# Expert weights: the low parts of every weight piece subtracted on VectorE instead of three in four there and one on GpSimd

## The chip, the core and the metric

One NeuronCore of one Trainium2 chip runs the whole program. The metric is the device time of one execution in microseconds (us). The engines are named as the profile names them: PE is TensorE's matmul, PEld its weight load, DVE is VectorE, ACT is ScalarE, POOL is GpSimd, and SP is SyncE, which here only issues DMAs.

## What is computed

The reference is a two-layer network in float32 on 1024 tokens of width 1024. The part around this change is the mixture of experts of the first layer: a router gives each token two of 32 experts, and each expert is a gated feed-forward net.

```python
hg = lax.ragged_dot(xs, w_gate.astype(xs.dtype), sizes)
hu = lax.ragged_dot(xs, w_up.astype(xs.dtype), sizes)
ys = lax.ragged_dot(jax.nn.silu(hg) * hu, w_down.astype(xs.dtype), sizes)
ys = ys * gates.reshape(-1)[order][:, None].astype(ys.dtype)
y = jax.ops.segment_sum(ys, tok, num_segments=t)
```

`xs` are the tokens of each expert in a row; `w_gate` and `w_up` are 1024 x 512 per expert, `w_down` is 512 x 1024. What comes before (two recurrent mixers, an output projection, the router) and after (the second layer) is not touched.

## The kernel before

**Exact products from rounded halves.** The matrix engine works on numbers in the rounded type F32R. To keep float32's accuracy each operand is split in two: a high part h, the raw number rounded to F32R, and a low part l = raw - h. `split` (lines 109 to 116) does it: ACT makes h by a copy (line 112), and another engine makes l by a subtraction (line 113). A product then takes three matmuls: h by h, h by l, l by h.

**One expert.** `expert` (from line 955) handles up to 128 tokens. POOL clears the tile `X` (line 960) and gathers the expert's tokens into it by an indirect DMA (line 961). PE transposes them (line 969), and `split` gives `XTh` and `XTl`. Each of the three weight matrices is used in four pieces of 512 KB. `wload` (lines 972 to 980) takes the next raw piece that has been loaded, and splits it into `ewh` and `ewl`, each 128 x 1024 with four buffers. Its argument q is the number of the piece in the matrix, 0 to 3. Pieces of the gate and up matrices feed six matmuls each (line 989), pieces of the down matrix too (line 1010). Between, ACT and DVE form silu(gate) * up in `eth` (lines 994 to 996), PE transposes it (line 1001) and it is split into `Hh` and `Hl`. At the end ACT scales the result into `Y` (line 1012), and POOL adds it to the tokens by an indirect DMA (line 1013).

**Who subtracts.** `wload` picks the engine by the piece's number: one of the four pieces of each matrix, three per expert and 96 in all, has its low part made on POOL, the other 288 on DVE.

```python
eng = nc.gpsimd if q == 1 else nc.vector
```

**The stage.** `moe` (from line 1018) runs the 32 experts as generators, one expert's down product beside the next one's gate and up products. The raw pieces are loaded by SP (line 376) in a ring: 19 buffers, seven of which (`eraw`) remain from expert 8 on; a buffer is loaded again when its piece has been split. From expert 8 on the freed memory serves `hyena_filters` (line 1154), work for the second layer that is done beside the experts: a small network's outputs are multiplied with a window on DVE (`hfb`, line 1217), POOL adds and subtracts pairs of them (`hsum`, line 1220, and `hd`, line 1223), the results are split (`hsh` on ACT, `hsl` on DVE, lines 115 and 116), transformed on PE (`dps`), combined on DVE (lines 1284 and 1285), and added and subtracted once more on POOL (`HR` and `HS`, line 1252).

**The order of the work.** No queue is written by hand: the program is recorded, and a scheduler that estimates every instruction sets the order on each engine at build time. A change of one instruction's engine can therefore move others on all five engines. Each engine then works its own queue strictly in order. A last part of `moe` for experts with more than 128 tokens is a loop on the chip that runs only where there are any.

Of the kernel before, what the change touches and what calls it, by code (L numbers as in the profile page):

```python
# [49 lines left out]
class Kern:  # L50
# [904 lines left out]
    def expert(self, ep, psm, pst, pg, gi, gate, wg, wu, wd, next_raw):  # L955


        nc = self.nc
        X = ep.tile([P, D], F32, name="X")
        nc.gpsimd.memset(X, 0.0)  # L960
        nc.gpsimd.indirect_dma_start(out=X, out_offset=None, in_=self.h2_d,
                                     in_offset=bass.IndirectOffsetOnAxis(ap=gi, axis=0),
                                     bounds_check=L - 1, oob_is_err=False)
        XTh = ep.tile([P, 8, P], F32R, name="XTh")
        XTl = ep.tile([P, 8, P], F32R, name="XTl")
        for q in range(2):
            pt = pst.tile([P, 4, P], F32, name="pt")
            for t in range(4):
                nc.tensor.transpose(pt[:, t], X[:, (q * 4 + t) * P:(q * 4 + t + 1) * P], self.ident)
            self.split(XTh[:, q * 4:q * 4 + 4], XTl[:, q * 4:q * 4 + 4], pt)  # L970

        def wload(w, q, down=False):
            shape = [P, D] if down else [P, 2, 512]
            eng = nc.gpsimd if q == 1 else nc.vector
            raw = next_raw(self.piece(w, q, down))
            h = ep.tile(shape, F32R, name="ewh", tag="ewh", bufs=4)
            l = ep.tile(shape, F32R, name="ewl", tag="ewl", bufs=4)
            self.split(h, l, raw, eng=eng)
            return h, l

        yield
        pgu = []
        for w in (wg, wu):
            ps = psm.tile([P, 512], F32, name="pgu", tag="s")
            for q in range(4):
                h, l = wload(w, q)
                for k in range(2):
                    for i, (a, b) in enumerate(((XTh, h), (XTh, l), (XTl, h))):
                        nc.tensor.matmul(ps, a[:, q * 2 + k], b[:, k], start=q == 0 and k == 0 and i == 0,  # L989
                                         stop=q == 3 and k == 1 and i == 2)  # L990
            pgu.append(ps)
            yield
        th = ep.tile([P, 512], F32, name="eth", bufs=1)
        nc.scalar.activation(th, pgu[0], AF.Tanh, scale=0.5)
        nc.vector.scalar_tensor_tensor(th, th, 1.0, pgu[0], op0=ALU.add, op1=ALU.mult)
        nc.vector.tensor_tensor(th, th, pgu[1], op=ALU.mult)
        Hh = ep.tile([P, 4, P], F32R, name="Hh", bufs=1)
        Hl = ep.tile([P, 4, P], F32R, name="Hl", bufs=1)
        pt = pst.tile([P, 4, P], F32, name="pt")
        for t in range(4):  # L1000
            nc.tensor.transpose(pt[:, t], th[:, t * P:(t + 1) * P], self.ident)
        self.split(Hh, Hl, pt)
        yield
        py = pg.tile([P, D], F32, name="g", tag="g")
        for q in range(4):
            h, l = wload(wd, q, True)
            for half in range(2):
                sl = slice(half * 512, half * 512 + 512)
                for i, (a, b) in enumerate(((Hh, h), (Hh, l), (Hl, h))):
                    nc.tensor.matmul(py[:, sl], a[:, q], b[:, sl], start=q == 0 and i == 0, stop=q == 3 and i == 2)  # L1010
        Y = ep.tile([P, D], F32, name="Y", bufs=1)
        nc.scalar.activation(Y, py, AF.Copy, scale=gate)
        nc.gpsimd.indirect_dma_start(out=self.x1_d, out_offset=bass.IndirectOffsetOnAxis(ap=gi, axis=0),
                                     in_=Y, in_offset=None, bounds_check=L - 1, oob_is_err=False,
                                     compute_op=ALU.add)
        yield
# [1285 lines left out]
```

## Time and profile before

| what | us |
|---|---|
| timed runs, median of 3 | 3980.1 |
| timed runs, lowest and highest | 3979.16 and 3992.83 |
| the profiled execution, its own time | 3969.92 |
| span of the profiled execution, first to last instruction | 3967.6 |

The profile is of the profiled execution, which took 2.3 us more than the span of its instructions and 10.2 us less than the median of the timed runs. Times in the rows count from the first instruction. Busy time is the time in which an engine has an instruction running, also where that instruction is held up; "idle before" is the time in which it had none, with what ended it. Durations of neighbouring instructions on DVE and ACT overlap by some hundredths of a us, so that sums of durations lie a few per cent above busy times. The experts' stage reaches from about 1140 us to about 1980 us; in it the experts 0 to 7 run until about 1380 us, the filters' work runs beside the experts from there to about 1900 us, and the last experts run alone again.

### The profile page before, as it was taken

How to read it: one execution, taken by the hardware profiler on the slowest of the kernel's cores; microseconds unless marked ns; L12 is line 12 of the kernel's file. 1: busy time of each engine (PE TensorE's matmuls, PEld its weight loads, DVE VectorE, ACT ScalarE, POOL GpSimd, SP SyncE). 2: the span in 40 equal slices, each digit the busy share in tenths (PEclk: the TensorE clock that was granted, in tenths of full speed). 3: DMA queues.
4: the chain of work that ended last, by engine and by line, in shares of the span. 5: the costliest groups of instructions: out<-in, count | busy, mean ns of one | idle time of the engine just before them, and what ended most of it. 6: DMA issues, size and time to landing. Idle time of an engine off the chain costs nothing. (4 is left out here: it accounts for less than half of the span.)

```text
span 3967.6 us, 52346 instructions
## 1 busy us (share of the span) xinstructions
PE 3544.1 (89%) x19799; PEld 2845.8 (72%) x19799; DVE 2861.4 (72%) x3992; ACT 1503.4 (38%) x2166; POOL 1540.5 (39%) x882
## 2 busy tenths in 40 slices
PE   6999897988978889999879999999776999999897
PEld 6888776666766667777656767887564777888775
DVE  7767858776457889998755887411995577777798
ACT  4332333433226766666633333222123213222331
POOL 4444434553015568777601222000771212223353
PEclk8999997899979999999989999999887999999998
DMA  4222224444568778888854777666556722222521
GB/s 102 96 85 107 97 74 148 137 151 145 182 208 285 233 247 287 294 268 274 280 153 132 213 207 194 185 192 220 161 170 195 258 103 69 85 75 95 177 94 69
DMA packets 540591, 669.34 MB, mean 169 GB/s; under 512 B 151819, under 2 KB 352015, under 8 KB 539824
## 3 DMA queue, kind: packets, MB, share of 16 engines
q1 hardware_dynamic: 429136, 535.38, 42.3%
q10 hardware_dynamic: 101984, 113.79, 8.4%
q0 software_dynamic: 9216, 16.81, 1.9%
q8 instruction: 157, 2.57, 0.3%
q14 instruction: 98, 0.80, 0.1%
HBM read 500.72 MB, written 181.83 MB: 172 GB/s over the span
## 5 line engine op out<-in xcount | busy, mean ns | idle before, releaser
L113 DVE TENSOR_TENSOR ewl<-eraw,ewh 128x1024 fp32r<-128x1024 f32 x243 | 398.8, 1658 | 40.6 <-ACT ewh L112 40.3
L112 ACT CAST ewh<-eraw 128x1024 fp32r<-128x1024 f32 x324 | 334.5, 1049 | 114.1 <-PE pgu L989 51.5
L125 PE MATMUL g<-x2h,wl 128*128 128x512 f32 x688 | 279.2, 406 | 0.0
L125 PE MATMUL g<-x2h,wh 128*128 128x512 f32 x688 | 278.9, 406 | 0.1
L125 PE MATMUL g<-x2l,wh 128*128 128x512 f32 x688 | 277.7, 404 | 0.0
L125 PE MATMUL g<-h,sw 128*128 128x512 f32 (+1 forms) x752 | 243.9, 401 | 20.5 <-ACT sw L112 9.6
L113 POOL TENSOR_TENSOR ewl<-eraw,ewh 128x1024 fp32r<-128x1024 f32 x81 | 215.3, 2658 | 111.1 <-ACT ewh L112 103.0
L163 POOL TENSOR_TENSOR sraw<-sraw 128x1024 f32<-128x1024 f32 x24 | 74.0, 3083 | 431.8 <-DVE sw L113 419.9
L125 PE MATMUL g<-xl,sw 128*128 128x512 f32 x616 | 241.5, 392 | 0.0
L989 PE MATMUL pgu<-ewl,XTh 128*128 128x512 f32 x512 | 210.5, 411 | 28.6 <-POOL ewl L113 18.0
L112 ACT CAST sw<-sraw 128x1024 fp32r<-128x1024 f32 x144 | 148.8, 1048 | 207.0 <-PE g L125 156.2
L125 PE MATMUL g<-z 128*128 128x512 f32 x820 | 201.7, 395 | 22.7 <-DVE z L113 19.7
L125 PE MATMUL g<-sw,h 128*128 128x256 f32 x960 | 184.6, 294 | 22.9 <-DVE sw L113 17.8
L989 PE MATMUL pgu<-ewh,XTh 128*128 128x512 f32 x512 | 204.2, 401 | 0.7 <-ACT XTh L112 0.7
L989 PE MATMUL pgu<-ewh,XTl 128*128 128x512 f32 x512 | 202.8, 396 | 0.0
L125 PEld LDWEIGHTS g<-z 128*128 128x128 f32 x820 | 155.1, 190 | 60.0 <-DVE z L113 23.0
L125 PEld LDWEIGHTS g<-h,sw 128*128 128x128 f32 (+1 forms) x752 | 143.2, 191 | 57.1 <-ACT sw L112 10.5
L113 DVE TENSOR_TENSOR wl<-raw,wh 128x1024 fp32r<-128x1024 f32 x43 | 52.6, 1223 | 173.1 <-ACT wh L112 167.7
L125 PEld LDWEIGHTS g<-sw,h 128*128 128x128 f32 x960 | 158.0, 202 | 23.9 <-DVE sw L113 18.6
L113 POOL TENSOR_TENSOR sw<-sraw,sw 128x1024 fp32r<-128x1024 f32 x39 | 102.5, 2628 | 179.9 <-ACT sw L112 179.9
L499 DVE SCALAR_TENSOR_TENSOR u<-sC,cw,u 128x1023 f32<-128x1023 f32 (+2 forms) x84 | 164.6, 1975 | 1.7 <-ACT u L497 1.4
L193 DVE TENSOR_TENSOR sC<-sU,g 128x512 f32<-128x512 f32 x140 | 95.2, 682 | 89.1 <-PE g L125 86.5
(684 smaller groups left out, 10113.7 us busy)
## 6 DMA issues: line engine op xcount, KB each, us to landing
eraw<-in_exp_w_down SPq DMA_DIRECT2D x112, 512.0 KB, 5.7
eraw<-in_exp_w_up SPq DMA_DIRECT2D x108, 512.0 KB, 4.7
eraw<-in_exp_w_gate SPq DMA_DIRECT2D x104, 512.0 KB, 5.6
sraw<-in_w_in SPq DMA_DIRECT2D x12, 2048.0 KB, 7.8
raw<-in_w_in ACTq DMA_DIRECT2D x43, 512.0 KB, 4.5
SC<-SC SPq DMA_DIRECT2D x32, 512.0 KB, 3.6
cSA<-X SPq DMA_DIRECT2D x32, 512.0 KB, 4.6
cSC<-SC SPq DMA_DIRECT2D x32, 512.0 KB, 7.6
```

What stands on the lines that cost most here:

```text
L112: nc.scalar.copy(h, raw)
L113: (eng or nc.vector).tensor_tensor(l, raw, f32(h), op=ALU.subtract)
L125: nc.tensor.matmul(ps, a, b, start=i == 0, stop=i == n - 1)
L163: Q(A11, A11, A21, op=ALU.subtract)
L193: V(c, x, ps, op=ALU.add)
L499: nc.vector.scalar_tensor_tensor(u[:, j:], x[:, :L - j], cw[:, ct, 3 - j:4 - j], u[:, j:], op0=ALU.mult, op1=ALU.add)
L989: nc.tensor.matmul(ps, a[:, q * 2 + k], b[:, k], start=q == 0 and k == 0 and i == 0, stop=q == 3 and k == 1 and i == 2)
```

## The change

`wload` no longer picks an engine: `split` is called without one, so that all four subtractions of each matrix go to DVE. Nothing else is edited.

```diff
         def wload(w, q, down=False):
             shape = [P, D] if down else [P, 2, 512]
-            eng = nc.gpsimd if q == 1 else nc.vector
             raw = next_raw(self.piece(w, q, down))
             h = ep.tile(shape, F32R, name="ewh", tag="ewh", bufs=4)
             l = ep.tile(shape, F32R, name="ewl", tag="ewl", bufs=4)
-            self.split(h, l, raw, eng=eng)
+            self.split(h, l, raw)
             return h, l
```

Line numbers behind it are lower by one in the changed kernel. The queues of all engines are the same as before up to the start of the experts and from the work after them on; what the scheduler ordered anew lies in the experts' stage.

Two places of the queues follow. The first is DVE's queue around one of the early experts, from its gate pieces to its `Hl` (the numbers tell one buffer's loading from another). Before:

```order
L113 TENSOR_TENSOR ewl<-eraw_9675,ewh 128x1024
L113 TENSOR_TENSOR ewl<-ahead_9699,ewh 128x1024
L113 TENSOR_TENSOR ewl<-ahead_9711,ewh 128x1024
L113 TENSOR_TENSOR XTl<-pt,XTh 128x512
L113 TENSOR_TENSOR ewl<-ahead_9724,ewh 128x1024
L113 TENSOR_TENSOR ewl<-ahead_9748,ewh 128x1024
L113 TENSOR_TENSOR ewl<-ahead_9760,ewh 128x1024
L113 TENSOR_TENSOR Hl<-pt,Hh 128x512
L995 SCALAR_TENSOR_TENSOR eth<-eth,pgu 128x512
L996 TENSOR_TENSOR eth<-eth,pgu 128x512
```

The same place of DVE's queue in the changed kernel:

```order
L113 TENSOR_TENSOR ewl<-eraw_9675,ewh 128x1024
L113 TENSOR_TENSOR ewl<-eraw_9687,ewh 128x1024
L113 TENSOR_TENSOR ewl<-ahead_9699,ewh 128x1024
L113 TENSOR_TENSOR ewl<-ahead_9711,ewh 128x1024
L113 TENSOR_TENSOR XTl<-pt,XTh 128x512
L113 TENSOR_TENSOR ewl<-ahead_9724,ewh 128x1024
L113 TENSOR_TENSOR ewl<-ahead_9736,ewh 128x1024
L113 TENSOR_TENSOR ewl<-ahead_9748,ewh 128x1024
L113 TENSOR_TENSOR ewl<-ahead_9760,ewh 128x1024
L113 TENSOR_TENSOR Hl<-pt,Hh 128x512
L994 SCALAR_TENSOR_TENSOR eth<-eth,pgu 128x512
L995 TENSOR_TENSOR eth<-eth,pgu 128x512
```

The second piece of each four (9687 and 9736) has come into DVE's queue in its turn; `XTl`, `Hl` and the two `eth` keep their places behind the fourth piece.

The second place is POOL's queue in the stretch in which the filters' work runs beside the experts. Before:

```order
L1220 TENSOR_TENSOR hsum<-hfb_13734,hfb_13738 128x256
L1013 DMA x_d<-Y,idx 1024x1024
L113 TENSOR_TENSOR ewl<-eraw_12725,ewh 128x1024
L1252 TENSOR_TENSOR HR<-daC 128x256 x2
L113 TENSOR_TENSOR ewl<-eraw_12774,ewh 128x1024
L1252 TENSOR_TENSOR HR<-dbC,dbS 128x256 x2
L113 TENSOR_TENSOR ewl<-eraw_12907,ewh 128x1024
L960 MEMSET X 128x1024
L1013 DMA x_d<-Y,idx 1024x1024
L961 DMA X<-h_d,idx 128x1024
```

The same place of POOL's queue in the changed kernel:

```order
L1219 TENSOR_TENSOR hsum<-hfb_13734,hfb_13738 128x256
L1012 DMA x_d<-Y,idx 1024x1024
L1251 TENSOR_TENSOR HR<-daC 128x256 x2
L960 MEMSET X 128x1024
L961 DMA X<-h_d,idx 128x1024
L1251 TENSOR_TENSOR HR<-dbC,dbS 128x256 x2
L1012 DMA x_d<-Y,idx 1024x1024
```

POOL keeps the filters' additions, the clearing of `X` and the two indirect DMAs of each expert, and these now stand directly behind one another.

## Rows read from the trace of the kernel before

**Rows 1.** The page, its lines of busy time: us, share of the span, number of instructions.

```profile
PE 3544.1 (89%) x19799; PEld 2845.8 (72%) x19799; DVE 2861.4 (72%) x3992; ACT 1503.4 (38%) x2166; POOL 1540.5 (39%) x882
```

**Rows 2.** Busy time by stretch, all instructions; the first row names the columns.

```profile
core 0: us, PE busy (x) PEld busy (x) DVE busy (x) ACT busy (x) POOL busy (x), PEclk, DMA share, GB/s
...
1170.00:1380.00 210.00, 179.41 (x751) 139.24 (x752) 166.45 (x142) 139.36 (x161) 109.03 (x53) 0.92 0.76 250
1380.00:1900.00 520.00, 485.01 (x2340) 377.40 (x2339) 477.36 (x481) 350.91 (x466) 387.55 (x243) 0.98 0.83 274
1900.00:1980.00 80.00, 69.44 (x317) 54.95 (x315) 57.67 (x52) 51.99 (x58) 45.67 (x21) 0.95 0.83 284
```

**Rows 3.** The same of `ewl` alone: PE, PEld, DVE, POOL, clock, DMA.

```profile
1170.00:1380.00 210.00, 88.31 (x209) 42.34 (x209) 120.83 (x77) 68.80 (x26) 0.92 0.76 250
1380.00:1900.00 520.00, 196.18 (x474) 90.26 (x473) 300.14 (x178) 156.76 (x60) 0.98 0.83 274
1900.00:1980.00 80.00, 35.44 (x86) 16.43 (x86) 47.17 (x32) 27.34 (x10) 0.95 0.83 284
```

**Rows 4.** One instruction's ns, least/median/most: the two engines' `ewl`.

```profile
L113 DVE TENSOR_TENSOR ewl<-eraw,ewh x243: 1202/1214/5149, 1192.0 to 1966.4; 128x1024 fp32r<-128x1024 f32 x122
L113 POOL TENSOR_TENSOR ewl<-eraw,ewh x81: 2343/2447/3454, 1192.0 to 1961.6; 128x1024 fp32r<-128x1024 f32 x81
```

**Rows 5.** The timeline of one early expert: start, us, engine, instruction, idle time before.

```profile
1269.53 1.21 DVE L113 TENSOR_TENSOR ewl<-eraw,ewh 128x1024 fp32r<-128x1024 f32 x1
1271.04 4.15 DVE L113 TENSOR_TENSOR ewl<-eraw,ewh 128x1024 fp32r<-128x1024 f32 x2 [0.30 <-ACT ewh L112]
1275.12 0.68 DVE L113 TENSOR_TENSOR Hl<-pt,Hh 128x512 fp32r<-128x512 f32 x1
...
1269.97 3.01 POOL L113 TENSOR_TENSOR ewl<-eraw,ewh 128x1024 fp32r<-128x1024 f32 x1
...
1275.85 0.50 PE L1010 MATMUL g<-ewh,Hl 128*128 128x512 f32 x1 [2.21 <-DVE Hl L113]
```

**Rows 6.** The timeline beside the filters' work, POOL and DVE.

```profile
1493.31 2.00 POOL L1252 TENSOR_TENSOR HR<-daC 128x256 f32<-128x256 f32 x2
1494.75 2.90 POOL L113 TENSOR_TENSOR ewl<-eraw,ewh 128x1024 fp32r<-128x1024 f32 x1
...
1494.02 4.73 DVE L113 TENSOR_TENSOR ewl<-eraw,ewh 128x1024 fp32r<-128x1024 f32 x1
```

**Rows 7.** `hsl` alone: its DVE busy time by stretch, and one's ns.

```profile
1380.00:1900.00 520.00, 51.93 (x182) 34.63 (x182) 58.93 (x64) 0.98 0.83 274
...
L116 DVE SCALAR_TENSOR_TENSOR hsl<-hsum,hsh x32: 406/604/3342, 1437.3 to 1846.6; 128x256 fp32r<-128x256 f32 x32
```

**Rows 8.** One instruction's ns: the `hsum` (`hd` alike), and `HR`, one of four such rows.

```profile
L1220 POOL TENSOR_TENSOR hsum<-hfb,hfb x32: 718/1584/2238, 1429.2 to 1845.4; 128x256 f32<-128x256 f32 x32
...
L1252 POOL TENSOR_TENSOR HR<-daC x16: 738/1516/1784, 1493.3 to 1876.0; 128x256 f32<-128x256 f32 x16
```

**Rows 9.** PE's waits from 1170 to 1980 us: total, times, longest.

```profile
PE pgu L989 <- POOL ewl L113: 18.0, 12, 5.6
PE g L1010 <- DVE Hl L113: 15.6, 7, 2.8
```

**Rows 10.** What SP's loads waited for from 1170 to 1980 us; POOL's scattered results.

```profile
SPq L376 <- POOL ewl L113: 159.0, 65, 7.5
...
L1013 POOL DMA_INDIRECT x_d<-Y,idx x32: 1561/1995/4905, 1215.1 to 1974.3; - x32
```

**Rows 11.** The timeline of ACT, one result `Y` per expert: experts 1, 6, 28, 30.

```profile
1237.80 1.12 ACT L1012 ACTIVATE Y<-g,gcol 128x1024 f32<-128x1024 f32 x1 [0.31 <-PE g L1010]
...
1351.87 1.11 ACT L1012 ACTIVATE Y<-g,gcol 128x1024 f32<-128x1024 f32 x1
...
1925.69 1.12 ACT L1012 ACTIVATE Y<-g,gcol 128x1024 f32<-128x1024 f32 x1 [0.54 <-PE g L1010]
...
1964.33 1.12 ACT L1012 ACTIVATE Y<-g,gcol 128x1024 f32<-128x1024 f32 x1
```

## The prediction

> **What bounds the kernel now.** The page comes first: over the whole span PE is busy 89%, DVE 72%, POOL 39% [rows 1]. Such averages say little, since the change touches one stage only. So the second view is busy time by stretch, in the three parts of the experts' stage: the early experts (1170 to 1380 us), the middle with the filters' work beside (1380 to 1900), the last experts (1900 to 1980). PE and DVE are high in all three and neither is full: 179.4 and 166.5 of 210 us, then 485.0 and 477.4 of 520, then 69.4 and 57.7 of 80 [rows 2]. The DMA engines are 0.76 to 0.83 busy, ACT at most 0.68. The stage is thus two engines in a chain, PE and DVE, which hold each other up, and in the middle DVE is near its limit: its 42.6 us without work there are spread over 481 instructions.
>
> Third, the same view for `ewl` alone: 26, 60 and 10 of the pieces were subtracted on POOL, and DVE's 77, 178 and 32 took 120.8, 300.1 and 47.2 us [rows 3]. Fourth, how long one takes: on DVE the median is 1.21 us, hardly over the least (1.20), but the longest took 5.15; on POOL it is 2.34 us at best and 2.45 in the median [rows 4]. So most of DVE's subtractions run undisturbed, and some stand still. The timeline says beside what. In an early expert POOL's subtraction runs from 1269.97 to 1272.98; two DVE subtractions that would take 2.4 us take 4.15, end at 1275.19, and `Hl`, queued behind them, makes PE wait 2.21 us [rows 5]. In the middle one DVE subtraction takes 4.73 us, while POOL does two additions for `HR` and then a weight piece, back to back [rows 6]. While one engine runs such an instruction on two SBUF operands, the other's stands.
>
> That is the question of this change: a weight piece on POOL is not free for DVE. What does it cost there, against the 1.21 us that it costs when DVE does it?
>
> **The change, part by part.**
>
> *Added on DVE.* 96 subtractions of 1.21 us: 31.5 us in the early stretch (26), 72.6 in the middle (60), 12.1 in the last (10); one more lies before 1170 us, and one at a border is counted on both sides.
>
> *Returned on DVE.* The lengthening is measured time less undisturbed time. Early: 120.8 - 77 x 1.21 = 27.6 us. Last: 47.2 - 32 x 1.21 = 8.5. Hardly anything else with two operands runs on POOL there, so I give all of it to the moved pieces. Middle: `ewl` 300.1 - 178 x 1.21 = 84.8, and `hsl` 58.9 - 64 x 0.41 = 32.7 [rows 7], together 117.5. This is shared with the filters' own additions on POOL: 32 `hsum`, 32 `hd` and 64 `HR` and `HS`, which hold for about 0.73 us each when nothing delays them [rows 8], 128 x 0.73 = 93 us, against 60 x 2.34 = 140 us of weight pieces. By held time the pieces have 60% of it, 70.5 us. The ends: by the medians, in which POOL's own waiting is counted (32 x 1.58, 32 x about the same, 64 x 1.52, against 60 x 2.45), their share is 42%, 50 us; at most it is all of `ewl`'s own lengthening, 84.8. I take 70.5, since held time is what DVE stands behind. A larger figure, all of the 117.5, is excluded because `HR` is seen at the start of the 4.73 us [rows 6].
>
> *Net on DVE.* Early +4, last +4, and middle 72.6 - 70.5 = **+2** (ends -12 and +23). Early and last DVE has 43.5 and 22.3 us without work, so the 4 us are covered; if that cover goes they are paid. In the middle I count the +2 in full.
>
> *PE's waits.* PE waited 18.0 us, 12 times, for a piece from POOL [rows 9]. A piece then comes after 1.21 us in DVE's queue instead of 2.4 to 3.0 on POOL, but the two pieces behind it are now later in that same queue. I take half, **-9 us** (ends 0 and -18).
>
> *`Hl` in the early experts.* Rebuilt from the timeline: the undisturbed queue runs the first piece to 1270.74, then three of 1.21 us to 1274.37; `Hl` starts there, not at 1275.12, 0.75 us sooner [rows 5]. PE waited for `Hl` 7 times, 15.6 us [rows 9]: 7 x 0.75 = **-5 us** (ends 0 and -15.6).
>
> *What costs nothing.* SP reloads a raw buffer when its piece is split, and waited 159 us for POOL to do so [rows 10]; these waits pass to DVE and get shorter, the loads are the same, and the DMA engines have a sixth to a quarter of their time over [rows 2]. POOL's clearing of `X`, its gathers and scatters and the filters' additions start earlier, since no piece stands before them; nothing that bounds waits for them. ACT gets two more activation-table loads by the new order, covered by its 169 us without work in the middle. The loop for large experts does not run: there are 32 scatters, one per expert [rows 10].
>
> **Sum:** +2 - 9 - 5 = -12 us. The profiled execution would go from 3969.9 to about 3958. It lies 10.2 us below the median of the timed runs, so against those runs I forecast 3980.1 - 12 = **3968 us**. Two independent terms, DVE's (-14, +21 about its value) and PE's (-20, +14), seldom meet their ends together; by the root of the sum of squares this case alone reaches from 3944 to 3993.
>
> **The rivals.**
>
> *Faster: the early experts reach the last ones' pace.* From expert 1 to 6 a result came every (1351.87 - 1237.80) / 5 = 22.8 us; from expert 28 to 30, with the same work and also nothing beside it, every 19.3 [rows 11]. If the early chain is held up by the lengthened subtractions alone, 7 experts gain 3.5 us each, 24.5, in place of the 5 for `Hl`: 3980.1 - 12 + 5 - 24.5 = 3949. For it: the granted clock, 0.92 there and 0.98 in the middle [rows 2], could rise when PE waits less. Against: the last experts had POOL's pieces too, and kept their pace. The Trainium skill, "SBUF — State Buffer", section "SBUF: two separate sides", calls the port pair that DVE and GpSimd share an exclusive lock, held for the whole instruction, behind which the other fully blocks. The trace agrees on the place, not on the amount: if each piece had cost DVE its whole 2.34 us, 140 us would return in the middle where at most 117.5 were lost, and then PE's 35 us without work there would be the most to win.
>
> *Slower: the filters' additions take the place of the weight pieces.* In the middle they lengthen DVE by 117.5 - 70.5 = 47 us now, 0.37 each. Without the pieces in POOL's queue they stand directly behind one another, and meet a DVE whose queue holds a third more subtractions. If every one of the 128 is paid in full, 93 us, DVE loses 46 more, and as it has little time over there the end moves by them: 3968 + 46 = 4014. It is slower than now by 0.5% from 32 us more than my sum, at 0.62 us for each addition. For it: back-to-back POOL instructions already starve a waiting DVE subtraction [rows 6]. Against: DVE also has instructions that read PSUM, beside which an addition runs unseen. A milder form has the same cause: if nothing at all came back, the middle would be charged 72.6 us against the 42.6 that DVE has there, 30 more, 3968 - 2 + 30 = 3996; I give it a twentieth, within this rival, since the lengthened rows are there to see. The Trainium skill, page "Perfetto Trace Analysis", section "Optimizing Scalar/DVE Operations", speaks for this form, and so against the change: where DVE is saturated, moving some of its work to ScalarE or even GpSimd may make sense. It adds that GpSimd and DVE share a read port, so that it might not help, and this caveat is what the trace bears out.
>
> *The change does nothing.* Excluded: the queues show 96 pieces moved.
>
> **How the numbers follow.** About 0.5%, 20 us, is what a measurement of this kernel can tell from no change: 3960 to 4000. My forecast has 0.58; a sixth of it lies below 3960 (0.10), nearly all the rest within. The faster rival has 0.24, of which 0.22 below 3960. The slower has 0.18, of which 0.13 reaches above 4000, and the forecast's upper end lends 0.01. Faster 0.32, same 0.54, slower 0.14. The range takes the forecast's own lower end, which lets out a tenth, and reaches to 4002, leaving a tenth of the slower rival above.
>
> **What would show it.** In the profile after: no `ewl` on POOL and 384 on DVE with a mean near 1.3 us in place of some 1.6; DVE's busy time in the stage within 20 us of before; a stage some 12 us shorter; `Hl`'s waits at about 1.4 us each. A mean of `hsl` still near 0.9, or `ewl` at 1.4 or more, would show the slower rival; 20 us per early expert the faster. My sum is wrong in its base if DVE's busy time falls or grows by over 25 us, and in its PE terms if PE's waits for `ewl` grow by what POOL's were.

## The result, and the profile after

The changed kernel took 3917.97 us in the median of four runs (3910.88 to 3923.73), the kernel before 3979.63 on the same chip: a ratio of **0.9852**, with a 95% interval from 0.9829 to 0.9876. That is 62 us less, or 49 to 68. The forecast was 12 us less, and the result lies below the low end of its range. The two profiled executions differ by less, 3921.0 against 3969.9 us, since that of before lies 10 us under its median and that of after 3 above; what follows accounts for their spans, 3919.2 against 3967.6, so for 48.4 us.

Where they went is read from ACT's timeline, by the result `Y` of the experts 0, 1, 6, 8, 28 and 31 of the changed kernel:

```profile
1210.03 1.12 ACT L1011 ACTIVATE Y<-g,gcol 128x1024 f32<-128x1024 f32 x1 [0.31 <-PE g L1009]
1230.15 1.12 ACT L1011 ACTIVATE Y<-g,gcol 128x1024 f32<-128x1024 f32 x1 [0.31 <-PE g L1009]
...
1333.31 1.10 ACT L1011 ACTIVATE Y<-g,gcol 128x1024 f32<-128x1024 f32 x1
...
1392.07 1.11 ACT L1011 ACTIVATE Y<-g,gcol 128x1024 f32<-128x1024 f32 x1 [0.27 <-PE g L1009]
...
1872.50 1.12 ACT L1011 ACTIVATE Y<-g,gcol 128x1024 f32<-128x1024 f32 x1 [0.57 <-PE g L1009]
...
1919.64 1.11 ACT L1011 ACTIVATE Y<-g,gcol 128x1024 f32<-128x1024 f32 x1 [4.95 <-DMA x_d<-Y,idx]
```

The same results came at 1213.7, 1237.8, 1351.9, 1407.3, 1925.7 and 1972.9 us before ([rows 11] show three of them). So 7.6 us are won by expert 1, 10.9 more from there to expert 6, and 38.0 from expert 8 to expert 28, where the filters' work runs beside; 3.3 are lost between experts 6 and 8, nothing changes over the last three, and the work behind the experts takes 4.9 longer. In other words, an early expert takes 20.6 us instead of 22.8, one in the middle 24.0 instead of 25.9.

The page's line of busy time, against [rows 1]:

```profile
PE 3538.9 (90%) x19799; PEld 2844.4 (73%) x19799; DVE 2834.2 (72%) x4088; ACT 1507.2 (38%) x2168; POOL 1289.0 (33%) x786
```

DVE has 96 instructions more, 116 us of undisturbed work, and is busy 27 us less. Busy time by stretch (columns as in [rows 2]; the middle now ends at 1840 us), all instructions, and below it `ewl` alone with PE, PEld and DVE:

```profile
1170.00:1380.00 210.00, 186.29 (x808) 143.34 (x808) 177.80 (x184) 153.87 (x175) 48.18 (x31) 0.95 0.81 270
1380.00:1840.00 460.00, 452.88 (x2202) 355.05 (x2203) 425.44 (x507) 335.08 (x440) 222.22 (x173) 0.99 0.89 299
```

```profile
1170.00:1380.00 210.00, 91.27 (x224) 43.54 (x224) 130.50 (x109) 0.95 0.81 270
1380.00:1840.00 460.00, 185.56 (x455) 86.43 (x455) 299.06 (x230) 0.99 0.89 299
```

In the middle, before, PE was without work for 35 of 520 us, 6.7% [rows 2]; now for 7.1 of 460, 1.5%. PE has become what bounds this stretch (the run with the piece left out, below, bears on this), and the DMA engines deliver 299 GB/s in place of 274. DVE's 230 subtractions there take 299.1 us, 1.30 each, against 300.1 us for 178, 1.69 each [rows 3]; in the early experts 1.20 against 1.57.

```profile
L113 DVE TENSOR_TENSOR ewl<-eraw,ewh x324: 1202/1218/1811, 1192.5 to 1914.9; 128x1024 fp32r<-128x1024 f32 x162
```

In ns of one, the longest of the `eraw` group fell from 5149 to 1811 [rows 4], the median stayed. `hsl` too is no longer held:

```profile
1380.00:1840.00 460.00, 44.79 (x159) 30.24 (x159) 28.02 (x56) 0.99 0.89 299
```

That is 0.50 us each, against 0.92 [rows 7]. PE's waits from 1170 us to the end of the stage in the changed kernel (total, times, longest), and under them ACT's for `hsum`:

```profile
PE g L1009 <- DVE Hl L113: 12.7, 10, 4.2
...
PE pgu L988 <- DVE ewl L113: 2.3, 2, 1.7
...
PE g L1009 <- DVE ewl L113: 0.4, 1, 0.4
```

```profile
ACT hsh L115 <- POOL hsum L1219: 6.0, 5, 2.3
```

Before, ACT's waits for `hsum` and PE's for low parts were these; PE waited not only for POOL [rows 9] but for DVE as well:

```profile
ACT hsh L115 <- POOL hsum L1220: 29.4, 18, 4.1
```

```profile
PE pgu L989 <- POOL ewl L113: 18.0, 12, 5.6
PE pgu L989 <- DVE ewl L113: 10.3, 12, 2.3
...
PE g L1010 <- DVE ewl L113: 2.2, 2, 1.9
PE g L1010 <- POOL ewl L113: 1.6, 3, 0.8
```

All together PE's 32.1 us went down to 2.7. ACT's waits for `hsum` fell from 29.4 to 6.0 us, those for `Hl` hardly, from 15.6 to 12.7.

### The profile page after: what moved, and what is told of

The parts are those of the page before. It is cut to its first block, busy times and chain, and to the rows that moved or that the text cites. A ratio compares the mean times of both kernels' runs of the same rounds, so it can differ in the third digit from the quotient of the medians.

```text
span 3919.2 us, 52350 instructions
## 1 busy us (share of the span) xinstructions
PE 3538.9 (90%) x19799; PEld 2844.4 (73%) x19799; DVE 2834.2 (72%) x4088; ACT 1507.2 (38%) x2168; POOL 1289.0 (33%) x786
## 5 line engine op out<-in xcount | busy, mean ns | idle before, releaser
L113 DVE TENSOR_TENSOR ewl<-eraw,ewh 128x1024 fp32r<-128x1024 f32 x324 | 415.7, 1306 | 41.6 <-ACT ewh L112 37.6
L125 PE MATMUL g<-z 128*128 128x512 f32 x820 | 201.6, 395 | 22.8 <-DVE z L113 19.7
L125 PE MATMUL g<-sw,h 128*128 128x256 f32 x960 | 185.0, 294 | 22.9 <-DVE sw L113 17.9
L125 PEld LDWEIGHTS g<-h,sw 128*128 128x128 f32 (+1 forms) x752 | 143.4, 191 | 57.5 <-ACT sw L112 10.5
L125 PEld LDWEIGHTS g<-sw,h 128*128 128x128 f32 x960 | 158.4, 202 | 24.0 <-DVE sw L113 18.7
L113 DVE TENSOR_TENSOR sw<-sraw,sw 128x1024 fp32r<-128x1024 f32 x105 | 136.7, 1316 | 34.8 <-ACT sw L112 33.9
L125 PEld LDWEIGHTS g<-x2h,wl 128*128 128x128 f32 x688 | 133.0, 193 | 38.3 <-issue 11.0
```

The costliest lines, as they stand in the source:

```text
L113: (eng or nc.vector).tensor_tensor(l, raw, f32(h), op=ALU.subtract)
L125: nc.tensor.matmul(ps, a, b, start=i == 0, stop=i == n - 1)
```

## The experiments

After the result three things could have carried the gain: that DVE no longer stands beside POOL's subtractions (**standing**), that the piece from POOL came late for PE (**late piece**), and that POOL's own queue is emptier for the filters' additions and the gathers (**queue**). A fourth was the new order that the scheduler made. Each ratio below is against the kernel before on the same chip, with its 95% interval; "changed" is the kernel after the edit.

**An idle subtraction on POOL.** All four pieces are DVE's, as in the changed kernel, and POOL subtracts as before, into a tile that nothing reads.

```diff
             self.split(h, l, raw)
+            if q == 1:
+                d = ep.tile(shape, F32, name="ewd", tag="ewd", bufs=1)
+                nc.gpsimd.tensor_tensor(d, raw, raw, op=ALU.subtract)
```

> The changed kernel, and beside it POOL subtracts each second raw piece from itself into a tile that nobody reads: 96 subtractions as long as the ones that the change took away, on two SBUF operands. All of DVE's subtractions stay on DVE. Theory 1 (standing still): what the change won is the time that DVE stands behind POOL's two-operand instructions. Then DVE's mean ewl goes from 1.31 back to 1.5 us or more, over 100 us of lengthening return on top of the 116 us that DVE now does, and the time comes back to 3980 or above. Theory 2 (the late piece): the win is that PE gets every piece from one queue 1.2 us after its turn, not 2.4 to 3 us late from POOL. No piece comes from POOL here, so the time stays at 3918 within 10 us. Theory 3 (POOL's own queue): the win is that gathers and the filters' additions no longer queue behind pieces. They queue again here, so most of the 62 us return, while DVE's subtractions need not lengthen.

4021.18 us, ratio 1.0107 (1.0074 to 1.0139): some 100 us above the changed kernel, more than the whole gain. DVE's `ewl` from 1140 to 2040 us:

```profile
L113 DVE TENSOR_TENSOR ewl<-eraw,ewh 128x1024 fp32r<-128x1024 f32 x324 | 491.8, 1549 | 15.2 <-ACT ewh L112 14.9
```

1549 ns in the mean, 1306 in the changed kernel, and PE waits for `ewl` from DVE again, 24 us. POOL's subtractions beside all 384 of DVE's cost more than the edit ever won; but POOL's queue is as full as before, so this run alone does not part standing from queue.

**POOL's queue filled with memsets.**

```diff
+            if q == 1:
+                for _ in range(3):
+                    nc.gpsimd.memset(raw, 0.0)
```

> The changed kernel, and POOL clears each second raw buffer three times after its piece is split: 288 memsets of about 0.95 us, 274 us of POOL's time, with no operand read. Theory 1 (standing still): a memset shares little with DVE; the time stays within 3913 to 3935. Theory 2 (the late piece): no piece comes later; 3918 within 10 us. Theory 3 (POOL's own queue): POOL is as full as before the change (255 us of pieces), gathers and additions wait as long, and 30 to 62 us return: 3948 to 3980.

3963.65 us, 0.9969 (0.9951 to 0.9988). DVE was held no more than in the changed kernel (mean 1302), yet most of the gain was gone. The edit did more than was meant: the three memsets keep the raw buffer longer than one subtraction does, and ACT waited 46.6 us for `eraw` from the DMA. Inconclusive; two later runs put the question better.

**Only the lateness.** DVE does every piece; then POOL touches it once more, with a memset of the raw tile and an addition on one column, so that PE has to wait for POOL.

```diff
+            if q == 1:
+                nc.gpsimd.memset(raw, 0.0)
+                l1 = l[:, :1] if down else l[:, 0, :1]
+                r1 = raw[:, :1] if down else raw[:, 0, :1]
+                nc.gpsimd.tensor_tensor(l1, f32(l1), r1, op=ALU.add)
```

> The changed kernel, but the low part of each second piece goes through POOL's queue once more: one memset of its raw buffer (about 0.95 us), then an addition of a cleared number to one column of the low part, so that PE gets the piece about 1.2 us after DVE has made it, as late as when POOL made it. POOL's long two-operand instructions stay away. Theory 1 (standing still): DVE is not held, 3913 to 3935. Theory 2 (the late piece): PE's waits for these pieces come back (19.6 us named on POOL before the change, and what followed from them), 3945 to 3980. Theory 3: a third of the former load on POOL's queue, 3925 to 3940.

3974.49 us, 0.9993 (0.9972 to 1.0014): all of the gain gone, though DVE is held no more than in the changed kernel. `ewl` on DVE, and PE's waits:

```profile
L113 DVE TENSOR_TENSOR ewl<-eraw,ewh 128x1024 fp32r<-128x1024 f32 x324 | 415.1, 1298 | 94.2 <-ACT ewh L112 41.2 <-issue 38.6 <-POOL HS L1256 4.5
```

```profile
PE pgu L993 <- POOL ewl L982: 48.2, 27, 7.5
...
PE g L1014 <- POOL ewl L982: 4.1, 5, 1.5
```

A late piece, with 152 us of POOL's queue taken as well, can thus cost as much as the whole change won. By the medians the delay is that of before: a memset of 0.95 us and an addition of 0.26 come behind DVE's subtraction, 1.21 us, where POOL's subtraction of before was 2.45 - 1.21 = 1.24 us later than DVE's [rows 4]. Its tail is long, though, since the addition is itself held at times; its mean is 0.65 us and its longest 4.07:

```profile
L982 POOL TENSOR_TENSOR ewl<-ewl,eraw x81: 183/262/4072, 1192.5 to 1964.7; 128x1 fp32r<-128x1 f32 x81
```

**The edit for the early experts alone.**

```diff
-            eng = nc.gpsimd if q == 1 else nc.vector
+            eng = nc.gpsimd if q == 1 and self.mid else nc.vector
...
+                self.mid = e >= 8
```

> The kernel before, with the change for the experts 0 to 7 alone; from expert 8 on, beside the filters' work, the second piece stays on POOL. Theories 1 and 2: the early experts keep the changed kernel's pace, 20.4 us instead of 22.8, and win about 18 us: 3962 of 3980, the middle stays as it was. Theory 3: POOL has no filters' additions early, so its queue matters only for the gathers; the win there would be below 8 us, and the larger part lies in the middle.

3967.29 us, 0.9971 (0.9953 to 0.9988). Early experts take 20.66 us each, as changed, and middle ones 26.26, close to the 25.9 of before: each stretch follows its own share of the edit. By this run the early experts hold a fifth of the gain (0.29% of 1.48%), by the changed kernel's own trace more, 18.5 of 48.4 us.

**One more buffer for the split pieces**, on the kernel before and on the changed one. If a late piece hurts because PE has none in hand, a fifth buffer should give the kernel before a third to a half of the gain.

```diff
-            h = ep.tile(shape, F32R, name="ewh", tag="ewh", bufs=4)
-            l = ep.tile(shape, F32R, name="ewl", tag="ewl", bufs=4)
+            h = ep.tile(shape, F32R, name="ewh", tag="ewh", bufs=5)
+            l = ep.tile(shape, F32R, name="ewl", tag="ewl", bufs=5)
...
-                fw4 = w.tile([64, 2, 256], F32, name="fw4")
+                fw4 = w.tile([64, 2, 256], F32, name="fw4", bufs=1)
```

> The kernel before, with five buffers instead of four for the high and the low parts of the pieces (the room comes from one buffer of the filters' weights fw4). POOL still makes three pieces of each expert. Theory 1 (standing still): DVE stands as long as before, 120 us beside POOL's pieces, so 3970 to 3980. Theory 2 (the late piece): with one more piece in store PE does not run out when one comes 1.2 us late; PE's waits for POOL's pieces (19.6 us) fall below 8 and a third to a half of the change's win comes without it, 3945 to 3960.

> The changed kernel with the same fifth buffer. Theory 1: DVE bounds the middle, more store gives it no time: 3910 to 3920. Theory 2: no late piece is left, so the store has nothing to cover either: 3908 to 3920. A larger gain, below 3900, would say that jitter of another kind (the waits for Hl, ACT's casts behind PE) still holds the chain up in the changed kernel.

On the kernel before 4027.36 us, 1.0099 (1.0066 to 1.0132): slower. PE's waits for POOL's pieces did fall to 7.3 us, but those for DVE's rose to 28.4, and the work behind the experts grew from 1994.7 to 2019.7. On the changed kernel 3913.85, 0.9819 (0.9787 to 0.9850): the experts end 21 us sooner, and the work behind them takes 2018.8 us instead of 1999.6. Both were ordered anew by the scheduler, so neither settles what a late piece costs.

**The queue filled again, with no raw buffer kept.** One column of the raw tile is copied, and three memsets go to a tile of their own.

```diff
+            if q == 1:
+                d = ep.tile([P, D], F32, name="ewd", tag="ewd", bufs=1)
+                nc.gpsimd.tensor_copy(d[:, :1], raw[:, :1] if down else raw[:, 0, :1])
+                for _ in range(3):
+                    nc.gpsimd.memset(d, 0.0)
```

> The second run again without its side effect (there the cleared raw buffers came free late, and ACT waited 46.6 us for loads): POOL copies one column of each second raw piece into a tile of its own and clears that tile three times. POOL is as full as before the change, no raw buffer is held, no piece comes late, DVE does not stand. Theories 1 and 2: 3915 to 3930. Theory 3 (POOL's own queue): the filters' additions and the gathers wait, ACT's waits for hsum go from 6 back to some 25 us, and 20 to 40 us return: 3938 to 3958.

3947.83 us, 0.9915 (0.9889 to 0.9941), so about 25 us above the changed kernel. ACT waits 22.5 us for the `hsum` again. By its expectation this is the queue's sign. POOL was filled with more than it had before, though, 359 us of memsets and copies against some 253 us of pieces [rows 3], so this is an upper figure for the queue.

**The filters' additions on DVE too.**

```diff
-                    nc.gpsimd.tensor_tensor(s_, hf[0], hf[1], op=ALU.add)
+                    nc.vector.tensor_tensor(s_, hf[0], hf[1], op=ALU.add)
...
-                    nc.gpsimd.tensor_tensor(hd[:, b], hf[0], hf[1], op=ALU.subtract)
+                    nc.vector.tensor_tensor(hd[:, b], hf[0], hf[1], op=ALU.subtract)
...
-        self.nc.gpsimd.tensor_tensor(out, x, y, op=op)
+        self.nc.vector.tensor_tensor(out, x, y, op=op)
```

> The changed kernel, with the filters' 128 additions and subtractions (hsum, hd, HR, HS) on DVE too. DVE gains 128 x 0.41 = 52 us of work and loses the 34 us that it still stands beside them: +18 us. Theory 1, with DVE as the bound of the middle: 3930 to 3940. Theory 2: the work comes from one queue in its turn, nothing waits for another engine: 3915 to 3930.

> The eighth run's kernel on the chip of the run before it, for the difference: 3900 to 3915, ratio about 0.981.

3908.97 us, 0.9808 (0.9781 to 0.9835), and in a second run of the same kernel 3906.91, 0.9839 (0.9801 to 0.9876). `ewl`'s mean falls to 1219 ns, which is the undisturbed value. By the ratios this kernel lies 5 to 23 us below the changed one, which was measured twice and on other chips; of the four pairs of intervals three overlap. So the additions that stay on POOL cost about that much at most, and a gain is not shown for certain. They do not take the pieces' place.

**The parts one by one.** Four kernels on one chip. The first leaves the disputed piece out: the low part of the second of every four weight pieces is a tile of zeros, which nobody computes. So DVE has the 288 subtractions of before and POOL none. In this kernel and the next two the four buffers of `ewl` serve three pieces of every four.

```diff
             h = ep.tile(shape, F32R, name="ewh", tag="ewh", bufs=4)
+            if q == 1:
+                nc.scalar.copy(h, raw)
+                return h, self.zl if down else self.zl.rearrange("p (k c) -> p k c", k=2)
```

The second adds to it POOL's subtraction, in place on the raw tile, for which nobody waits but the next load (standing and queue, without a late piece). The third puts memsets of like length in its stead (queue alone). The fourth is the changed kernel again.

```diff
                 nc.scalar.copy(h, raw)
+                nc.gpsimd.tensor_tensor(raw, raw, raw, op=ALU.subtract)
```

```diff
                 nc.scalar.copy(h, raw)
+                for _ in range(2):
+                    nc.gpsimd.memset(raw, 0.0)
+                nc.gpsimd.memset(raw[:, :512] if down else raw[:, 0], 0.0)
```

> A floor for the decomposition. The low part of every second piece is left out: nobody subtracts it, and PE multiplies with a tile of zeros in its place (as many matmuls as ever). DVE has 9 subtractions per expert as before the change, POOL none. Kernel before = this + POOL's queue being full + DVE standing beside POOL + the piece coming late; changed kernel = this + 116 us of work on DVE. All theories: below the changed kernel's 3918; with DVE as the bound of the middle 3840 to 3880, with PE as the bound 3885 to 3910.

> The floor, and POOL subtracts each second raw piece from itself in place, after ACT's copy: the same length and two operands as the kernel before, the raw buffer held as long, but nobody waits for the result. Against the kernel before only the late piece is missing. Theory 1 (standing still): 3965 to 3985, as the kernel before. Theory 2 (the late piece): at most 3950. Theory 3 (POOL's own queue): equal to the next run within 10 us.

> The floor, and POOL clears each second raw buffer two and a half times after ACT's copy, 2.4 us, as long as its subtraction was, with no operand read. Theory 1: within 10 us of the floor. Theory 2: within 10 us of the floor. Theory 3: 20 to 40 us above the floor.

> The changed kernel on the chip of the three runs of the decomposition, so that the differences are taken on one chip: 3910 to 3925, ratio 0.985 within 0.003.

| kernel | us | ratio (95%) |
|---|---|---|
| before | 3972.16 | 1 |
| piece left out | 3911.26 | 0.9855 (0.9830 to 0.9881) |
| left out, POOL's memsets | 3917.94 | 0.9863 (0.9844 to 0.9882) |
| left out, POOL's subtraction | 3942.54 | 0.9932 (0.9913 to 0.9951) |
| changed | 3921.86 | 0.9866 (0.9842 to 0.9890) |

The steps between the rows, with intervals from resampling the timed runs: POOL's queue 6.7 us (-4.5 to 13.7), DVE standing **24.6** (19.8 to 31.6), the piece that PE has to wait for **29.6** (20.8 to 35.8); they are the 60.9 us from the floor (the kernel with the piece left out) to the kernel before. The changed kernel lies 10.6 us (-2.3 to 18.7) above the floor: that is all that 116 us of added work on DVE cost. So on this chip the edit wins 50.3 us, where 62 were measured first (44 to 63 by this ratio, 49 to 68 by the first). The profiled executions agree on the steps: from the result of expert 0 to that of expert 31 they took 690.9 us in the floor, 699.4 with the memsets, 728.4 with the subtraction and 759.3 before, in steps of 8.5, 29.0 and 30.9; the changed kernel took 709.5. By its expectation the floor would have come out at 3840 to 3880 us if DVE bounded the middle, and at 3885 to 3910 if PE did; it came out at 3911.

The steps are not pure. The scheduler ordered each of these kernels anew, and that is in every step. The third step is what is left between the kernel with POOL's idle subtraction and the one before, so it holds all that hangs on the piece being POOL's, the buffers of `ewl` too. It also holds some standing: DVE's 288 subtractions took 474 us in the kernel before, 443 beside the idle ones and 367 in the floor, so that 31 of the 107 us of lengthening came back only in the third step. And in the kernel with memsets ACT waited 27 us for raw pieces, 9 in the floor, which makes the first step rather too large and the second too small. Standing is thus likely worth more than 24.6 us, and the late piece less than 29.6. Nor are the prices fixed: POOL's idle subtractions cost 31 us on top of the floor, queue and standing together, but some 100 us in the first experiment, beside 384 subtractions on DVE. What a queue as full as before costs beside 384 was not measured.

The mechanism stands in `ewl`'s rows from 1140 to 2040 us, of the kernel with the piece left out, with the memsets, with the subtraction, and of the kernel before:

```profile
L113 DVE TENSOR_TENSOR ewl<-eraw,ewh 128x1024 fp32r<-128x1024 f32 x243 | 311.7, 1302 | 77.2 <-ACT ewh L112 75.2 <-issue 0.6 <-PE pgu L991 0.6
```

```profile
L113 DVE TENSOR_TENSOR ewl<-eraw,ewh 128x1024 fp32r<-128x1024 f32 x243 | 311.6, 1294 | 90.9 <-ACT ewh L112 88.7 <-DMA eraw<-in_exp_w_up 1.1
```

```profile
L113 DVE TENSOR_TENSOR ewl<-eraw,ewh 128x1024 fp32r<-128x1024 f32 x243 | 379.6, 1583 | 48.8 <-ACT ewh L112 47.9 <-DMA eraw<-in_exp_w_up 0.7
```

```profile
L113 DVE TENSOR_TENSOR ewl<-eraw,ewh 128x1024 fp32r<-128x1024 f32 x243 | 398.8, 1658 | 40.6 <-ACT ewh L112 40.3
```

POOL's memsets of the same length leave DVE's 243 subtractions as they are, POOL's subtractions lengthen them by 68 us, and in the kernel before they are 87 us longer. And the middle by stretch, of the kernel with the piece left out and of the changed one in its second run:

```profile
1380.00:1840.00 460.00, 460.00 (x2317) 369.62 (x2316) 371.28 (x471) 342.24 (x458) 211.01 (x182) 1.00 0.90 306
```

```profile
1380.00:1840.00 460.00, 451.87 (x2192) 353.79 (x2192) 425.35 (x506) 335.38 (x441) 220.55 (x171) 0.99 0.89 298
```

With the piece neither late nor on POOL, PE is busy for all of the 460 us, at a granted clock of 1.00. DVE's busy time grows by 54 us from the one to the other, and PE loses 8.

**The scheduler's order taken out.** Both kernels without the scheduler's reordering. The queues should then differ by the 96 subtractions alone. By the two traces they are much closer than with the scheduler, but not that close: apart from `ewl`, DVE's other instructions stand in another order in 17 places, ACT's in 33 and POOL's in 11, all of them behind the result of expert 5.

```diff
-    with tile.TileContext(nc, schedule_with_timeline_sim=True) as tc:
+    with tile.TileContext(nc, schedule_with_timeline_sim=False) as tc:
```

> The kernel before, with the scheduler's reordering off: every queue stands in the order in which the program is written. It is the base of the next run; its time will be far from 3980, since all stages lose their order (4100 to 5500).

> The changed kernel in program order, so that against the run before it nothing moves but the 96 subtractions. If what the change wins is DVE's standing still and the late piece, it wins here too, 25 to 80 us. If most of the win is the scheduler's new order, it wins less than 10 us here or loses.

Before 4105.41 us, 1.0334 (1.0295 to 1.0373); changed 4023.64, 1.0137 (1.0097 to 1.0176). The edit wins 81.8 us here (73 to 99), more than with the scheduler. From the result of expert 1 to that of expert 5 every queue is the same but for the moved subtractions, and there an expert takes 17.9 us instead of 20.6:

```profile
1273.68 1.12 ACT L1012 ACTIVATE Y<-g,gcol 128x1024 f32<-128x1024 f32 x1 [0.31 <-PE g L1010]
...
1355.98 1.12 ACT L1012 ACTIVATE Y<-g,gcol 128x1024 f32<-128x1024 f32 x1 [0.31 <-PE g L1010]
```

```profile
1263.10 1.12 ACT L1011 ACTIVATE Y<-g,gcol 128x1024 f32<-128x1024 f32 x1 [0.31 <-PE g L1009]
...
1334.57 1.12 ACT L1011 ACTIVATE Y<-g,gcol 128x1024 f32<-128x1024 f32 x1 [0.31 <-PE g L1009]
```

So the early experts need no new order for their gain. For the middle a share of the order is not excluded, and what it added or took within the 62 us was not measured. PE's longest group of waits for low parts, in the first and in the second:

```profile
PE g L1010 <- DVE ewl L113: 41.7, 23, 2.0
```

```profile
PE pgu L988 <- DVE ewl L113: 4.6, 4, 1.8
```

In the first PE waited mostly for DVE's own pieces, which had been held beside POOL's (mean 1737 ns, 1260 in the changed one), and only 10.5 us for POOL's: standing on DVE turns into waits of PE.

**The same in the first stage.** The filters' additions on DVE as above, and 39 low parts of the input projection moved from POOL to DVE.

```diff
-                for blocks, Cs in self.strassen(pg, fr, wr, p, load, operand, first, tok, 4, (4, 5, 3)):
+                for blocks, Cs in self.strassen(pg, fr, wr, p, load, operand, first, tok, 4, ()):
```

> The run with the filters' additions on DVE, and in the first stage (the input projection) the three weight splits of seven that POOL makes there (39 subtractions) go to DVE as well. There DVE stands about 40 us beside them and would do 47 us more; PE is 94% busy and the subtractions feed it. By the two causes found (standing still, a late piece) 10 to 25 us fewer than the eighth run's 3909, 3884 to 3899; if PE bounds that stage, 3905 to 3912.

3893.86 us, 0.9804 (0.9767 to 0.9841), 13.0 us (8.3 to 17.3) below the same kernel without the last edit on that chip. It is the quickest kernel measured here. From 100 to 690 us DVE is busy 451 us instead of 438 with 46 instructions more, POOL 162 instead of 251.

## Why the prediction was wrong, point by point

- **The reading of the stage** held in part: two engines in a chain, with subtractions on DVE that stand while POOL runs one. That DVE is near its limit in the middle did not hold. `ewl`'s mean came out near the 1.3 us forecast, and no `ewl` is left on POOL.
- **Net on DVE** is the step that failed. It added up DVE's work, +72.6 and -70.5 in the middle, and charged the +2 to the end, as if DVE bounded that stretch. Its amounts were fair: DVE's busy time over the span moved by -27 us, just beyond the 25 named as the limit, so 143 us came back for 116 added, where 107 were forecast. But a us of added work and a us of standing have not the same price. Work that DVE does while PE is fed costs little: 10.6 us (-2.3 to 18.7) for 116. Standing falls on whatever is in the queue at that moment, and PE is often the one that waits for it: 24.6 us, rather more than less. By the steps of the four kernels DVE's net is thus -14 us instead of +2, the late piece with `Hl` up to -29.6 instead of -14, and POOL's queue -6.7 instead of nothing: -50 instead of -12. DVE's busy time near its limit [rows 2] hid this, because standing is counted in it: without the 117.5 us of lengthening it was busy about 360 of 520 us.
- **PE's waits**, forecast at -9, are the mis-sized term: the step that holds the late piece is worth 29.6 us (20.8 to 35.8). Half of the 18.0 us [rows 9] was taken, on the thought that the pieces behind would come later in DVE's queue. PE did not wait longer for them. Its waits for DVE's pieces, 12.5 us for which the prediction had no term, went down as well, so the waits for low parts fell by 29.4 of 32.1 us.
- **`Hl`**: forecast -5, by the waits -2.9. In one early expert it went as rebuilt, and further: the queue runs through almost without a hold and PE waits 0.65 us instead of 2.21 [rows 5]. Over the stage the waits were 1.27 us each, where 1.4 was named, but there were 10 in place of 7.

```profile
1260.83 5.18 DVE L113 TENSOR_TENSOR ewl<-eraw,ewh 128x1024 fp32r<-128x1024 f32 x4
...
1265.92 0.68 DVE L113 TENSOR_TENSOR Hl<-pt,Hh 128x512 fp32r<-128x512 f32 x1
```

```profile
1266.66 0.50 PE L1009 MATMUL g<-ewh,Hl 128*128 128x512 f32 x1 [0.65 <-DVE Hl L113]
```

- **What costs nothing**: for POOL's emptier queue this was not quite so. ACT's waits for `hsum` fell by 23 us, and filling the queue costs 6.7 us on top of the floor, which is not told apart from nothing, and at most some 25 beside all 384 subtractions.
- **The faster rival** came halfway: an early expert takes 20.6 us, neither 22.8 nor 19.3. The objection to it, that PE's 35 us without work in the middle would be the most to win, came nearest: 38.0 us were won between experts 8 and 28. That was luck in part, since it was tied to 2.34 us returned on DVE for each piece, and 143 us for 96 pieces are 1.5.
- **The slower rival** did not come. `hsl` fell to 0.50 us where 0.9 was its sign, and with the additions on DVE as well 5 to 23 us were won, which is not shown for certain. DVE's instructions that read PSUM were indeed not held: the 64 `XTl` took 669 to 692 ns in the kernel before. Its mild form, in which nothing returns, was contradicted by the rows that the prediction itself read.

The Trainium skill, "SBUF — State Buffer", section "SBUF: two separate sides", lets DVE with two SBUF inputs be blocked "only against a GpSimd op that reads SBUF". The runs agree: memsets 1294 ns, subtractions 1583, against 1302 with neither.

## What to carry to other kernels

Before work is moved onto an engine that looks full, take out of its busy time what is only standing still, and ask which engine is really fed too late: a piece that comes a us late to the engine that bounds can cost more than a us of work on one that does not. Work on two SBUF operands on POOL has three prices, its own time, DVE's hold and its lateness, and here the two that do not stand in POOL's row made up 54 of the 61 us between the floor and the kernel before. To price them apart, leave the disputed operation out, then put back one effect at a time, and look in each trace whether only that effect came back.

## What was not expected of the hardware

- POOL stands beside DVE too, and is not let in between. In the kernel with the late piece POOL's addition on a single column took 0.18 us at the least. One took 4.07, while DVE ran four instructions on two SBUF operands back to back; it ended when the last of them did, at 1407.7 us:

```profile
1403.65 4.07 POOL L982 TENSOR_TENSOR ewl<-ewl,eraw 128x1 fp32r<-128x1 f32 x1
```

```profile
1403.05 1.21 DVE L1193 SCALAR_TENSOR_TENSOR fa<-fn,fa 64x1024 f32<-64x1024 f32 x1
1404.19 2.35 DVE L113 TENSOR_TENSOR ewl<-eraw,ewh 128x1024 fp32r<-128x1024 f32 x2
1406.46 1.21 DVE L1194 SCALAR_TENSOR_TENSOR fa<-fn,fa 64x1024 f32<-64x1024 f32 x1
```

- Without the scheduler's reordering the experts' stage itself is quicker than with the scheduler: in the changed kernel 642 us from expert 1 to expert 31 against 689, 18.3 us per early expert, while the rest of the program loses more than that. Why, and whether the two can be joined, was not tried.
